# Gate rows of an mLSTM brought to all partitions by transfers from a DRAM scratch instead of matmuls

## The chip, the cores and the metric

One core of a Trainium2 chip runs the whole program. The metric is the device time of one execution in microseconds; a lower time is better.

## What is computed

The reference is a two-layer encoder trunk on 512 tokens of width 1024. Layer 0 mixes tokens with an mLSTM (a chunked, stabilised matrix memory with four heads), layer 1 with causal pooling; each layer then attends to 256 memory tokens and applies a squared-ReLU MLP, and every sub-layer ends in a LayerNorm. The change touches the mLSTM of layer 0 alone. Cut to that:

```python
def mlstm_chunk_step(carry, inp):          # per chunk; q, k, v, input gate, log forget gate
    b = jnp.cumsum(lf, axis=-1)
    dmat = jnp.where(tril, b[..., :, None] - b[..., None, :] + ig[..., None, :], -jnp.inf)
    m_t = jnp.maximum(b + m[..., None], jnp.max(dmat, axis=-1))
    wts = jnp.exp(dmat - m_t[..., None])
    sc = jnp.einsum('bhtd,bhsd->bhts', q, k) * wts
    num = jnp.einsum('bhts,bhsv->bhtv', sc, v) + ...      # the carried state
    h = num / jnp.maximum(jnp.abs(den), jnp.exp(-m_t))[..., None]
```

The kernel does not carry a state over chunks: for each head it forms the whole lower triangle of scores between 512 source and 512 target tokens. So each score needs a weight, the exponential of a number that belongs to the target token (a row, equal on all partitions) plus a number that belongs to the source token (a column, one value for each partition).

## The kernel before

All products run as three matmuls of float32r halves (`mm3`, lines 195 to 200: high by high, high by low, low by high). A weight unit of 128 by 1024 is loaded by SyncE (`unit`, lines 149 to 161), cast to its high half by ScalarE (line 159, tile `wh`), and the rest is found by VectorE (line 160, tile `wl`). There are five buffers each for `wh` and `wl`, and three for the raw loads.

The mLSTM stage begins with nine warm-up matmuls, then `pg`, the gate projection (line 350), then the projections for q and k, `conv(c)` (line 360), each with 24 matmuls, a causal convolution of four taps on ScalarE and VectorE (lines 363 to 365, tile `ac`), a SiLU and a split. Projections for v (`token_proj`, tiles `v`) alternate with the convolutions in the loop over (5, 2, 6, 3, 7): v of token tile 0, then conv(5), v of tile 1, conv(2), v of tile 2, conv(6), and so on. The four units of a v projection stay in their buffers through four token tiles, so that one buffer of five is left for the units of the convolutions in between.

Around these, smaller work is put in by due times: `defer(us, fn)` and `chain(us, step, fns)` (lines 175 to 181) count TensorE time as the program is written out, and `tick` calls what has come due. The order that results is a priority: each engine has its own queue, and the framework that writes the queues out may take a later instruction first where it expects an earlier one not to be ready. Each queue is then run in order.

- `gates()` (line 444), due at 5, makes the input gate and the log forget gate as rows on four partitions (one for each head). For each of the four token tiles s it then makes a segment of the target rows: a running sum (line 458), the source values (line 459), the subtraction of the stabiliser (line 460), and a split into high and low half in `rseg[s]` on partitions 0 to 3 and 32 to 35 (lines 461 and 462). The segments have 512, 384, 256 and 128 columns (`SEG`).
- `columns()` (line 464), due at 21, turns the source values and the stabiliser into columns by eight small transposes (`gcol`, `emcol`).
- `scores(h)` (line 379) has for each s a `weights(s)` and a `part(s)`. `weights(s)` brings row h of the segment to all 128 partitions by a matmul with a selecting matrix (line 385, PSUM tile `pb`; the matrix `sel` is loaded, cast and kept in a buffer of the pool `t2`). VectorE adds the column to the first 128 columns (line 388), GpSimd masks these (line 389), and ScalarE takes the exponential of them (line 390) and of the rest, straight out of PSUM (line 392). `part(s)` makes the scores (PSUM tile `pS`, pool `aux` with two buffers), and VectorE multiplies them by the weights (line 403); a split follows (lines 404, 405). The order is weights 0, weights 1, part 0, weights 2, part 1, weights 3, part 2, part 3, at steps of 2 (head 3: 2.2).
- The `rseg` tiles lie in the four buffers of the pool `lnp`, which the LayerNorm rows of layer 0 use next (`ln_load(0, 0)`, loaded by SyncE).

Of the kernel before, what the change touches and what calls it, by code (L numbers as in the profile page):

```python
# [9 lines left out]
F32 = mybir.dt.float32  # L10
F32R = mybir.dt.float32r
AF = mybir.ActivationFunctionType
ALU = mybir.AluOpType
AX = mybir.AxisListType

P = 128
D = 1024
S = 512
NT = S // P
KC = D // P  # L20
M = 256
H = 4
# [8 lines left out]
SIDE = dict(vkv="left", t5="left", hid="left", t2="right", rawd="right")  # L31
SEG = [S - P * s for s in range(NT)]
OFF = [sum(SEG[:s]) for s in range(NT)]
WU = 1024
LN_T = 7.2


def f32(ap):
    return ap.bitcast(F32)
# [3 lines left out]
def trunk(ctx: ExitStack, tc: tile.TileContext, a: dict, out: bass.AP):  # L43
    nc = tc.nc
    V, A, G, T = nc.vector, nc.scalar, nc.gpsimd, nc.tensor
# [13 lines left out]
    lnp_p = pool("lnp", 1, side="right")  # L59
    st_p = pool("st", 3, side="right")  # L60
    dram_p = pool("dram", 1, space=bass.MemoryType.DRAM)
    acc_p = pool("acc", 4, space=bass.MemoryType.PSUM)
    tmp_p = pool("tmp", 2, space=bass.MemoryType.PSUM)
# [4 lines left out]
    scoped = {}  # L68
# [20 lines left out]
    def ld(dst, src):  # L89
        nc.sync.dma_start(dst, src)  # L90
# [58 lines left out]
    def unit(src):  # L149
# [4 lines left out]
        else:  # L154
            r = raw_p.tile([P, WU], F32, tag="raw", name=f"raw{n}")
        ld(r, src)
        h = wh_p.tile([P, WU], F32R, tag="wh", name=f"wh{n}")
        l = wl_p.tile([P, WU], F32R, tag="wl", name=f"wl{n}")
        A.copy(h, r)  # L159
# [15 lines left out]
    def defer(us, fn):  # L175

        later.append([us, fn])
# [33 lines left out]
    def tok(t):  # L211
        return slice(t * P, (t + 1) * P)
# [122 lines left out]
    for q in range(4):  # L335
        r = vkv(f"xr{q}", F32)[:, : 2 * S].rearrange("p (z t) -> p z t", z=2)
        for z in range(2):
            k = 2 * q + z
            ld(r[:, z], a["xT"][:, k])
            h, l = x0.k(k)  # L340
# [37 lines left out]
    def scores(h):  # L378

        ws = {}  # L380

        def weights(s):
            n = SEG[s]
            pb = tmp_p.tile([P, 512], F32, tag="tmp", name=f"pb{h}{s}")
            T.matmul(pb[:, :n], sel[:, h], rseg[s], start=True, stop=True)
            gc = gcol[:, s, h : h + 1]
            w = ws[s] = t2(f"w{h}{s}", n)
            V.tensor_scalar(w[:, :P], pb[:, :P], gc, None, op0=ALU.add)
            G.affine_select(w[:, :P], w[:, :P], pattern=[[1, P]], compare_op=ALU.is_ge, fill=-1e30, base=0, channel_multiplier=-1)
            A.activation(w[:, :P], w[:, :P], AF.Exp)  # L390
            if n > P:
                A.activation(w[:, P:], pb[:, P:n], AF.Exp, bias=gc, scale=1.0)

        def part(s):
            if s == 0:
                sc[h] = t5(f"sh{h}", F32R), t5(f"sl{h}", F32R)
            w = ws[s]
            q, k = qk_k(h)
            n = SEG[s]
            sh, sl = (z[:, OFF[s] : OFF[s] + n] for z in sc[h])  # L400
            pS = aux_p.tile([P, 512], F32, tag="aux", name=f"pS{h}{s}")
            mm3(pS[:, :n], (k[0][:, tok(s)], k[1][:, tok(s)]), (q[0][:, s * P :], q[1][:, s * P :]), start=True, stop=True)
            V.tensor_tensor(w, pS[:, :n], w, ALU.mult)
            A.copy(sh, w)
            V.tensor_tensor(sl, w, f32(sh), ALU.subtract)

        fns = []
        for s in range(NT):
            fns += [lambda s=s: weights(s), lambda s=s: part(s)]
        order = (0, 2, 1, 4, 3, 6, 5, 7)  # L410
        return [fns[n] for n in order]
# [12 lines left out]
    ld(gateb, a["gateb"])  # L424
    w_v = h_units(a["w_v"][0])
    ident = const_tile("ident", [P, P])
    sel_f = scoped["t2"].tile([P, H, P], F32, tag="t2", name="sel_f")
    ld(sel_f, a["sel"])
    sel = scoped["t2"].tile([P, H, P], F32R, tag="t2", name="sel")
    A.copy(sel, sel_f)  # L430

    ga, gb, bc = t5("ga"), t5("gb"), t5("bc")
    i_r, lf = ga[0:4, 0:512], ga[0:4, 512:1024]
# [3 lines left out]
    m_r, gs_r = gb[0:4, 0:512], gb[0:4, 512:1024]  # L437
    gcol = const.tile([P, NT, H], F32, name="gcol")
    emcol = const.tile([P, NT, H], F32, name="emcol")

    seg = [bc[0:4, OFF[s] : OFF[s] + SEG[s]] for s in range(NT)]
    rseg = [lnp_p.tile([P, 512], F32R, tag=z, name=f"r{z}")[:, : SEG[s]] for s, z in enumerate(("g0", "g1", "b0", "b1"))]

    def gates():
        A.copy(lf, pg[64:68])
        V.scalar_tensor_tensor(i_r, pg[0:4], gateb[0:4], lf, ALU.add, ALU.add)
        A.copy(fe, pg[96:100])
        V.scalar_tensor_tensor(fp, pg[fs], gateb[fs], fe, ALU.add, ALU.add)
        A.activation(fa, fp, AF.Abs)
        A.activation(fe, fa, AF.Exp, scale=-1.0)  # L450
        A.activation(fe, fe, AF.Ln, bias=one_t[fs], scale=1.0)
        V.tensor_scalar(fa, fp, 0.0, None, op0=ALU.min)
        V.tensor_tensor(lf, fa, fe, ALU.subtract)
        V.tensor_tensor_scan(m_r, lf, i_r, 0.0, ALU.add, ALU.max)
        for r in rseg:
            G.memset(f32(r), 0.0)
        for s in range(NT):
            V.tensor_tensor_scan(seg[s], lf[:, s * P :], lf[:, s * P :], 0.0, ALU.add, ALU.bypass)
            V.tensor_tensor(gs_r[:, tok(s)], i_r[:, tok(s)], seg[s][:, :P], ALU.subtract)
            V.tensor_tensor(seg[s], seg[s], m_r[:, s * P :], ALU.subtract)  # L460
            A.copy(rseg[s][0:4], seg[s])
            V.tensor_tensor(rseg[s][32:36], seg[s], f32(rseg[s][0:4]), ALU.subtract)

    def columns():
        pc = tmp_p.tile([P, 512], F32, tag="tmp", name="pc")
# [3 lines left out]
        V.tensor_copy(gcol.rearrange("p a b -> p (a b)"), pc[:, 0:16])  # L469
        A.activation(emcol.rearrange("p a b -> p (a b)"), pc[:, 16:32], AF.Exp, scale=-1.0)  # L470

    defer(5, gates)
    defer(21, columns)
    for j, c in enumerate((5, 2, 6, 3, 7, None, None, None)):
        hf, t = j // 4, j % 4
# [3 lines left out]
        for q in range(2):  # L479
            h = 2 * hf + q  # L480
# [7 lines left out]
    b1 = const_tile("b1", [P, DEPTH, DFF // P])  # L488
# [12 lines left out]
    def head(h):  # L501
# [5 lines left out]
        for t in range(NT):  # L507
            pa = acc_p.tile([P, 512], F32, tag="acc", name=f"pa{h}{t}")
            pn.append(pa)
            for s in range(t + 1):  # L510
                o = OFF[s] + (t - s) * P
                mm3(pa[:, :258], (sh[:, o : o + P], sl[:, o : o + P]), (vh[h][:, s], vl[h][:, s]), start=s == 0, stop=s == t)
# [58 lines left out]
    for q in range(2):  # L571
        r = raw_p.tile([P, 4, M], F32, tag="raw", name=f"mr{q}")
# [84 lines left out]
    for i in range(DEPTH):  # L657
# [255 lines left out]
        for q in range(3, 4):  # L913
            n = f"{i}{q}"
# [24 lines left out]
def _layout(inp):  # L939
    c = np.ascontiguousarray  # L940

    def feat(w):

        k, n = w.shape
        return c(w.reshape(k // P, P, n // P, P).transpose(2, 1, 0, 3)).reshape(n // P, P, -1)

    def half(w):

        k, n = w.shape
        return c(w.reshape(4, 2, P, n // 512, 512).transpose(3, 0, 2, 1, 4)).reshape(n // 512, 4, P, 1024)  # L950

    x, mem = inp["x"][0], inp["mem"][0]
    w_in = inp["mlstm_w_in"][0]
    wg = np.zeros((D, 36), w_in.dtype)
    wg[:, 0:4] = w_in[:, 3072:3076]
    wg[:, 32:36] = w_in[:, 3076:3080]
    gb = np.zeros((36, 1), w_in.dtype)
    gb[0:4, 0] = inp["mlstm_gate_b"][0, 0:4]
    gb[32:36, 0] = inp["mlstm_gate_b"][0, 4:8]
    sel = np.zeros((P, H, P), np.float32)  # L960
    for h in range(H):
        sel[h, h] = 1.0
        sel[32 + h, h] = 1.0
    band = np.zeros((P, 2, 4, BAND), np.float32)
    for w, win in enumerate(WINDOWS):
        for s in range(P):
            for t in range(s, min(s + win, BAND)):
                band[s, 0, w, t] = np.float32(1.0) / np.float32(min(t + 1, win))
                band[s, 1, w, t] = np.float32(1.0 / win)
            band[s, :, w, s] -= np.float32(1.0)  # L970
    w1, w2 = inp["mlp_w1"], inp["mlp_w2"]
    return {
        "ident": np.eye(P, dtype=np.float32),
        "sel": sel,
        "band": band,
        "xT": c(x.T.reshape(KC, P, S).transpose(1, 0, 2)),
        "x": c(x.reshape(NT, P, D).transpose(1, 0, 2)),
        "memT": c(mem.T.reshape(KC, P, M).transpose(1, 0, 2)),
        "w_qk": feat(w_in[:, :1024]),
        "w_v": half(w_in[:, 1024:2048]),  # L980
        "w_o": half(w_in[:, 2048:3072]),
        "wg": c(wg.reshape(KC, P, 36).transpose(1, 0, 2)),
        "gateb": gb,
        "convw": c(inp["mlstm_conv_w"][0].reshape(4, KC, P).transpose(2, 1, 0)),
        "normg": c(inp["mlstm_norm_g"][0].reshape(KC, P).T),
        "w_out": half(inp["mlstm_w_out"][0]),
        "w_pool": c(inp["pool_w"][0].reshape(2, 2, 2, P, 256).transpose(0, 3, 1, 2, 4)).reshape(2, P, 1024),
        "pool_scale": c(inp["pool_scale"]),
        "w_k": feat(inp["mem_w_kv"][:, :D]),
        "w_kvv": half(inp["mem_w_kv"][:, D:]),  # L990
        "w_q": np.stack([feat(w) for w in inp["xattn_wq"]]),
        "w_ao": np.stack([half(w) for w in inp["xattn_wo"]]),
        "w1": np.stack([feat(w) for w in w1]),
        "b1": c(inp["mlp_b1"].reshape(DEPTH, DFF // P, P).transpose(2, 0, 1)),
        "w2": np.stack([np.stack([half(w[q * D : (q + 1) * D]) for q in range(4)]) for w in w2]),
        "b2": c(inp["mlp_b2"]),
        "ln_g": c(inp["ln_g"]),
        "ln_b": c(inp["ln_b"]),
    }
# [18 lines left out]
```

## Time and profile before

| | us |
|---|---|
| three runs | 1207.62, 1210.26, 1210.73 |
| median of the runs | 1210.26 |
| the profiled execution | 1208.14 |
| its span, first to last instruction | 1206.4 |
| TensorE busy in the span | 1191.3 |
| VectorE, ScalarE, GpSimd busy | 835.8, 577.7, 8.9 |

The page gives busy times and the chain of work that ended last. In the timeline of TensorE, matmuls are pipelined: what one costs is the distance from its start to the next start, not its duration. A bracket after a row tells how long the engine stood idle before it and what released it. SyncE issues all loads and stores; GpSimd issues none.

### The profile page before, as it was taken

The page shows a single profiled execution, that of the slowest core. Times are in us where ns is not written, and L with a number is a line of the kernel's source. Part 1 is how long each engine was busy: PE and PEld are TensorE (multiplying, and loading weights), DVE is VectorE, ACT ScalarE, POOL GpSimd, SP SyncE. Part 2 cuts the span into 40 slices and gives each one's busy share as a digit, 9 for nine tenths or more (in the row PEclk, how much of TensorE's full clock was granted, in tenths as well). Part 3 has the DMA queues.
Part 4 walks back from the last instruction along what each step waited for, and adds up shares of the span by engine and source line. Part 5 has one row for each costly group of instructions (what it writes and reads, how often), then busy time and mean ns, then how long its engine had stood idle before and what let it go on. Part 6 is the DMA issues. An engine that isn't in the chain of part 4 may idle for free.

```text
span 1206.4 us, 15476 instructions
## 1 busy us (share of the span) xinstructions
PE 1191.3 (99%) x6121; PEld 1017.5 (84%) x6121; DVE 835.8 (69%) x1145; ACT 577.7 (48%) x853; POOL 8.9 (1%) x35
## 2 busy tenths in 40 slices
PE   9899999999999999999999999999999999999997
PEld 6788889889888988888888889998898888888886
DVE  6776366485548775585698699874868459479746
ACT  6586585233423564454544444562356445454420
POOL 0000000000000000000000000000000000000000
PEclk9999999999999999999999999999999999999999
DMA  7132347624232416116105555544331512511311
GB/s 253 49 117 87 98 131 255 216 89 156 71 140 70 141 44 201 54 50 198 48 10 186 189 194 193 175 123 160 96 112 58 186 53 73 172 35 57 118 53 70
DMA packets 43177, 144.21 MB, mean 120 GB/s; under 512 B 5216, under 2 KB 5472, under 8 KB 43104
## 3 DMA queue, kind: packets, MB, share of 16 engines
q1 hardware_dynamic: 43104, 143.22, 36.2%
q8 instruction: 48, 0.79, 0.3%
q14 instruction: 25, 0.20, 0.0%
HBM read 136.91 MB, written 6.29 MB: 119 GB/s over the span
## 4 chain that ended last, share of the span: by engine, by line
PE 93%; DVE 3%; ACT 1%; DMA 1%; issue 0%; SPq 0%; DVEq 0%; ACTq 0%
PE h L196 10%; PE h L197 10%; PE h L198 10%; PE m L196 7%; PE m L198 7%; PE m L197 7%; PE ao L198 2%; PE ao L196 2%; PE ao L197 2%; PE q L196 2%; PE q L197 2%; PE q L198 2%; PE p L196 2%; PE p L198 2%; PE p L197 2%; PE mo L196 1%
## 5 line engine op out<-in xcount | busy, mean ns | idle before, releaser
L160 DVE TENSOR_TENSOR wl<-raw,wh 128x1024 fp32r<-128x1024 f32 x175 | 213.0, 1222 | 170.6 <-ACT wh L159 168.6
L159 ACT CAST wh<-raw 128x1024 fp32r<-128x1024 f32 x175 | 183.1, 1049 | 281.7 <-PE h L197 74.0
L843 DVE TENSOR_TENSOR b<-b,b 128x1024 f32<-128x1024 f32 x48 | 58.6, 1220 | 0.4
L196 PE MATMUL h<-xm00h,wh 128*128 128x512 f32 (+1 forms) x144 | 52.9, 367 | 0.0
L196 PE MATMUL h<-xm10h,wh 128*128 128x512 f32 (+1 forms) x144 | 52.8, 367 | 0.0
L196 PE MATMUL h<-xm01h,wh 128*128 128x512 f32 (+1 forms) x144 | 52.8, 367 | 0.0
L196 PE MATMUL h<-xm11h,wh 128*128 128x512 f32 (+1 forms) x144 | 52.8, 367 | 0.0
L197 PE MATMUL h<-xm00l,wh 128*128 128x512 f32 (+1 forms) x144 | 52.7, 366 | 0.0
L197 PE MATMUL h<-xm10l,wh 128*128 128x512 f32 (+1 forms) x144 | 52.7, 366 | 0.0
L198 PE MATMUL h<-xm01h,wl 128*128 128x512 f32 (+1 forms) x144 | 52.6, 365 | 0.0
L198 PE MATMUL h<-xm11h,wl 128*128 128x512 f32 (+1 forms) x144 | 52.6, 365 | 0.0
L198 PE MATMUL h<-xm00h,wl 128*128 128x512 f32 (+1 forms) x144 | 52.6, 365 | 0.0
L197 PE MATMUL h<-xm01l,wh 128*128 128x512 f32 (+1 forms) x144 | 52.6, 365 | 0.0
L197 PE MATMUL h<-xm11l,wh 128*128 128x512 f32 (+1 forms) x144 | 52.6, 365 | 0.0
L198 PE MATMUL h<-xm10h,wl 128*128 128x512 f32 (+1 forms) x144 | 52.6, 365 | 0.0
L815 ACT ACTIVATE r<-h,b 128x512 f32<-128x512 f32 x48 | 32.8, 682 | 0.0
L247 ACT ACTIVATE rs<-mv,eps_t 128x1 f32<-128x1 f32 x24 | 7.1, 295 | 53.5 <-DVE mv L245 53.5
L816 ACT ACTIVATE s<-r 128x512 f32<-128x512 f32 x48 | 30.3, 632 | 1.3
L196 PEld LDWEIGHTS h<-xm00h,wh 128*128 128x128 f32 x144 | 27.2, 189 | 4.5 <-ACT r L759 0.2
L197 PEld LDWEIGHTS h<-xm10l,wh 128*128 128x128 f32 x144 | 27.2, 189 | 4.4
L197 PEld LDWEIGHTS h<-xm00l,wh 128*128 128x128 f32 x144 | 27.1, 188 | 4.5
L197 PEld LDWEIGHTS h<-xm01l,wh 128*128 128x128 f32 x144 | 27.2, 189 | 4.4
(946 smaller groups left out, 3527.8 us busy)
## 6 DMA issues: line engine op xcount, KB each, us to landing
raw<-in_w SPq DMA_DIRECT2D x88, 512.0 KB, 3.8
b<-in_w SPq DMA_DIRECT2D x48, 512.0 KB, 4.3
raw<-in_w_q SPq DMA_DIRECT2D x24, 512.0 KB, 4.3
raw<-in_w_ao SPq DMA_DIRECT2D x16, 512.0 KB, 3.5
raw<-in_w_v SPq DMA_DIRECT2D x8, 512.0 KB, 6.0
raw<-in_w_o SPq DMA_DIRECT2D x8, 512.0 KB, 4.2
raw<-in_w_k SPq DMA_DIRECT2D x8, 512.0 KB, 4.2
raw<-in_w_kvv SPq DMA_DIRECT2D x8, 512.0 KB, 4.6
```

What stands on the lines that cost most here:

```text
L159: A.copy(h, r)
L160: V.tensor_tensor(l, r, f32(h), ALU.subtract)
L196: T.matmul(out_, l[0], r[0], start=start, stop=False)
L197: T.matmul(out_, l[0], r[1], start=False, stop=False)
L198: T.matmul(out_, l[1], r[0], start=False, stop=stop)
L247: A.activation(rs, mv[:, 1:2], AF.Sqrt, bias=eps_t, scale=1.0)
L815: A.activation(r, ps, AF.Relu, bias=b1[:, i, 8 * q + m : 8 * q + m + 1], scale=1.0)
L816: A.activation(s[m // 4][:, m % 4], r, AF.Square)
L843: V.tensor_tensor(d, u, v, op)
```

## The change

The rows no longer pass TensorE. `gates()` ends with the stabiliser; what follows for a segment is now `gate_rows(s)`, without the split into halves, and ends with a transfer of the segment (four partitions) into a DRAM scratch `rows`, issued on GpSimd's queue. The five functions are due one by one at 5, 8.5, 12, 15.5 and 19. `weights(s)` fetches row h of the segment 128 times out of the scratch into its buffer `w`, again on GpSimd's queue; the mask follows there, and one exponential with the column as its bias takes the whole width. The matrix `sel`, its load, its cast and its buffer are gone, as are the `rseg` tiles, their clearing on GpSimd, `pb` and its PSUM buffers.

```diff
 def weights(s):
     n = SEG[s]
-    pb = tmp_p.tile([P, 512], F32, tag="tmp", name=f"pb{h}{s}")
-    T.matmul(pb[:, :n], sel[:, h], rseg[s], start=True, stop=True)
-    gc = gcol[:, s, h : h + 1]
     w = ws[s] = t2(f"w{h}{s}", n)
-    V.tensor_scalar(w[:, :P], pb[:, :P], gc, None, op0=ALU.add)
+    G.dma_start(w, rows[h : h + 1, OFF[s] : OFF[s] + n].broadcast_to([P, n]))
     G.affine_select(w[:, :P], w[:, :P], pattern=[[1, P]], compare_op=ALU.is_ge, fill=-1e30, ...)
-    A.activation(w[:, :P], w[:, :P], AF.Exp)
-    if n > P:
-        A.activation(w[:, P:], pb[:, P:n], AF.Exp, bias=gc, scale=1.0)
+    A.activation(w, w, AF.Exp, bias=gcol[:, s, h : h + 1], scale=1.0)
...
-sel_f = scoped["t2"].tile([P, H, P], F32, tag="t2", name="sel_f")
-ld(sel_f, a["sel"])
-sel = scoped["t2"].tile([P, H, P], F32R, tag="t2", name="sel")
-A.copy(sel, sel_f)
...
-rseg = [lnp_p.tile([P, 512], F32R, tag=z, name=f"r{z}")[:, : SEG[s]] for s, z in enumerate(("g0", "g1", "b0", "b1"))]
+rows = dram_p.tile([H, SUM], F32, name="rows")

 def gates():
...
     V.tensor_tensor_scan(m_r, lf, i_r, 0.0, ALU.add, ALU.max)
-    for r in rseg:
-        G.memset(f32(r), 0.0)
-    for s in range(NT):
-        V.tensor_tensor_scan(seg[s], lf[:, s * P :], lf[:, s * P :], 0.0, ALU.add, ALU.bypass)
-        V.tensor_tensor(gs_r[:, tok(s)], i_r[:, tok(s)], seg[s][:, :P], ALU.subtract)
-        V.tensor_tensor(seg[s], seg[s], m_r[:, s * P :], ALU.subtract)
-        A.copy(rseg[s][0:4], seg[s])
-        V.tensor_tensor(rseg[s][32:36], seg[s], f32(rseg[s][0:4]), ALU.subtract)
+
+def gate_rows(s):
+    V.tensor_tensor_scan(seg[s], lf[:, s * P :], lf[:, s * P :], 0.0, ALU.add, ALU.bypass)
+    V.tensor_tensor(gs_r[:, tok(s)], i_r[:, tok(s)], seg[s][:, :P], ALU.subtract)
+    V.tensor_tensor(seg[s], seg[s], m_r[:, s * P :], ALU.subtract)
+    G.dma_start(rows[:, OFF[s] : OFF[s] + SEG[s]], seg[s])
...
-defer(5, gates)
+chain(5, 3.5, [gates] + [lambda s=s: gate_rows(s) for s in range(NT)])
 defer(21, columns)
```

## Rows read from the trace of the kernel before

**Rows 1.** The page: busy time, share of the span, instructions; then the chain by engine.

```profile
PE 1191.3 (99%) x6121; PEld 1017.5 (84%) x6121; DVE 835.8 (69%) x1145; ACT 577.7 (48%) x853; POOL 8.9 (1%) x35
...
PE 93%; DVE 3%; ACT 1%; DMA 1%; issue 0%; SPq 0%; DVEq 0%; ACTq 0%
```

**Rows 2.** What TensorE waited for, whole span: us in total, times, longest.

```profile
PE qk L198 <- DVE wl L160: 3.6, 2, 3.2
...
PE k L196 <- DVE k0l L206: 0.5, 1, 0.5
```

**Rows 3.** TensorE in order of time, 28 to 66 us: start, duration, instruction, [idle before].

```profile
45.97 0.50 PE L196 MATMUL v<-wh,x00h 128*128 128x512 f32 x1
49.64 0.80 PE L198 MATMUL qk<-x00h,wl 128*128 128x512 f32 x1 [3.16 <-DVE wl L160]
...
53.30 0.40 PE L198 MATMUL qk<-x00h,wl 128*128 128x512 f32 x1
```

**Rows 4.** Busy time of each engine, granted clock, DMA share, GB/s, after the wait.

```profile
49.60:53.30 3.70, 3.66 (x9) 2.91 (x10) 2.17 (x5) 2.88 (x5) 0.00 (x0) 0.56 0.40 144
```

**Rows 5.** VectorE by line, 36 to 50 us: count, busy us, mean ns, idle before.

```profile
L458 DVE TENSOR_TENSOR_SCAN bc<-ga 4x512 f32<-4x512 f32 (+3 forms) x4 | 3.1, 796 | 0.0
...
L460 DVE TENSOR_TENSOR bc<-bc,gb 4x512 f32<-4x512 f32 (+3 forms) x4 | 1.9, 472 | 0.1
...
L462 DVE TENSOR_TENSOR rg<-bc,rg 4x512 fp32r<-4x512 f32 (+1 forms) x2 | 1.1, 611 | 0.0
L459 DVE TENSOR_TENSOR gb<-ga,bc 4x128 f32<-4x128 f32 x4 | 1.1, 268 | 0.0
L462 DVE TENSOR_TENSOR rb<-bc,rb 4x256 fp32r<-4x256 f32 (+1 forms) x2 | 0.7, 348 | 0.1
```

**Rows 6.** VectorE in order of time, 10 to 60 us.

```profile
48.37 1.21 DVE L160 TENSOR_TENSOR wl<-raw,wh 128x1024 fp32r<-128x1024 f32 x1
...
57.32 1.22 DVE L160 TENSOR_TENSOR wl<-raw,wh 128x1024 fp32r<-128x1024 f32 x1 [4.85 <-ACT wh L159]
```

**Rows 7.** ScalarE in order of time, 10 to 60 us.

```profile
39.82 1.05 ACT L159 CAST wh<-raw 128x1024 fp32r<-128x1024 f32 x1
```

**Rows 8.** TensorE in order of time around the broadcast matmul of 128 columns.

```profile
74.88 0.22 PE L385 MATMUL pb<-rb,sel 128*128 128x128 f32 x1
...
75.22 0.39 PE L197 MATMUL qk<-x00l,wh 128*128 128x512 f32 x1
```

**Rows 9.** TensorE, 28 to 66 us: first matmuls of conv(6), the first broadcast matmul.

```profile
60.80 0.39 PE L196 MATMUL qk<-x00h,wh 128*128 128x512 f32 x1
...
64.20 0.39 PE L385 MATMUL pb<-rg,sel 128*128 128x512 f32 x1
64.43 0.39 PE L196 MATMUL qk<-x01h,wh 128*128 128x512 f32 x1
```

**Rows 10.** VectorE in order of time, 60 to 170 us.

```profile
66.89 0.35 DVE L388 TENSOR_SCALAR w<-pb,gcol 128x128 f32<-128x128 f32 x1 [1.90 <-PE pb L385]
...
75.59 0.55 DVE L403 TENSOR_TENSOR w<-pS,w 128x384 f32<-128x384 f32 x1
...
117.10 0.35 DVE L388 TENSOR_SCALAR w<-pb,gcol 128x128 f32<-128x128 f32 x1
...
120.13 0.29 DVE L403 TENSOR_TENSOR w<-pS,w 128x128 f32<-128x128 f32 x1 [1.98 <-PE pS L198]
```

**Rows 11.** GpSimd in order of time, 0 to 300 us.

```profile
65.21 0.29 POOL L389 TENSOR_SCALAR_AFFINE_SELECT w<-w 128x128 f32<-128x128 f32 x1 [51.63 <-DVE w L388]
...
72.15 1.15 POOL L389 TENSOR_SCALAR_AFFINE_SELECT w<-w 128x128 f32<-128x128 f32 x1 [4.55 <-DVE w L388]
```

**Rows 12.** SyncE's loads of LayerNorm rows, 128 copies of 2 KB: from issue to landing.

```profile
DMA to landing us min/median/max: 3.7/5.1/6.1
```

**Rows 13.** Chain that ended last, 163 to 180 us: start, duration, what.

```profile
165.88 1.13 DVE meml L576
...
167.04 4.62 DMA raw<-in_w_k
```

More of the change, by code (lines that the diff above doesn't have):

```diff
@@ L33 @@
 OFF = [sum(SEG[:s]) for s in range(NT)]
+SUM = sum(SEG)
 WU = 1024
@@ L959, in _layout @@
     gb[32:36, 0] = inp["mlstm_gate_b"][0, 4:8]
[L960 to L963, printed above, removed]
     band = np.zeros((P, 2, 4, BAND), np.float32)
@@ L973, in _layout @@
         "ident": np.eye(P, dtype=np.float32),
-        "sel": sel,
         "band": band,
```

## Prediction

> **What bounds the kernel now.** I read the page first: TensorE is busy for 1191.3 of 1206.4 us and makes 93% of the chain that ended last, against 835.8 us for VectorE [rows 1]. So a microsecond counts only if it is TensorE's own, or if TensorE stands still for it. The second view is therefore the list of TensorE's waits. It is short: the longest entry, 3.6 us in two pieces, is a matmul of a `conv` that waits for line 160, the low half of its weight unit [rows 2]. The third view is the order of time around the longer piece, and there the reader is to see two things. TensorE starts a matmul at 45.97, then stands still for 3.16 us and starts again at 49.64. Then it is slow: from 49.64 to 53.30 it starts nine matmuls, 3.66 us where nine at the usual distance of 0.23 [rows 9] take 2.07 [rows 3]. The mean granted clock there is 0.56, the lower of the two levels (1.2 instead of 2.4 GHz) for most of the stretch [rows 4]. So this one wait costs 3.16 + 1.59 = 4.75 us.
>
> Fourth, who was late? ScalarE cast the high half of that unit, conv(2)'s, at 39.82, done at 40.87 [rows 7]; VectorE began the low half only at 48.37 [rows 6]. In those 7.5 us VectorE worked nearly without a gap, mostly on the gates: four segments, each a running sum, two subtractions and the low half of `rseg`, all due at one moment ahead of that unit [rows 5]. The wait of TensorE is the gates' doing, and the edit to the gates matters more than the matmuls it was written beside.
>
> **The matmuls.** Sixteen of line 385 go, four for each head, of 512, 384, 256 and 128 columns. One of 512 occupies TensorE for 0.23 us, from 64.20 to 64.43 [rows 9]. At that rate 384 are 0.17 and 256 are 0.115. One of 128 and its successor together take 0.34, from 74.88 to 75.22, where the successor alone takes 0.23; so it costs 0.11 [rows 8]. A head is 0.23 + 0.17 + 0.115 + 0.11 = 0.62, four heads are **2.5 us**, all on the path, since TensorE does not wait once between 60 and 163 us.
>
> **The gates.** Ahead of conv(2)'s unit VectorE loses, first, the four subtractions of line 462, 1.1 + 0.7 = 1.8 us [rows 5]. Second, conv(2)'s unit is written out when 24 matmul triples of v, conv(5) and v have passed, 3 x 8 x 0.64 = 15.4 on the kernel's own count, so the parts due at 15.5 and 19 (segments 2 and 3) now come behind it. The mean segment is 0.80 + 0.47 + 0.27 = 1.54 us [rows 5], two are 3.1; these are the short ones, and by columns they have 384 of 1280, 0.3 x 6.1 = 1.8. I take 2.3. Together 4.1 us: the low half starts at 44.3 instead of 48.37 and ends at 45.5, about 1 us before TensorE ran dry at 46.47 (45.97 + 0.50) [rows 3]. So the wait should go, and with it the slow matmuls: **4.75 us**. What is late next there is `columns()`, whose transposes need all four segments and sit in TensorE's own queue; and the convolution's taps (line 365) share VectorE with it. I give back 0.4 us for that, between 0 and the 3.16 of the old wait, near the other piece of the same wait (3.6 - 3.2) [rows 2].
>
> **What is added.** Twenty transfers on GpSimd's queue. No row shows one issued there. From below, GpSimd's time for one is nothing that matters; from above it is like its slowest instruction, 1.15 us [rows 11]. The nearest row for the landing is SyncE's loads of LayerNorm rows, also 128 copies of 2 KB out of one row: 3.7 to 6.1, median 5.1 us [rows 12]; the shorter ones may be faster. After the landing come the mask (0.29 us for 128 columns [rows 11]) and one exponential of up to 512 columns (between that 0.29 and the 1.05 of a cast of 1024 [rows 7]; I take 0.7), so, with 0.3 for the issue, about 6.4 us from issue to use. How long was there? From line 388 to the multiplication of line 403 I count sixteen pairs, the shortest 3.0 us (117.10 to 120.13), the longest 8.7 (66.89 to 75.59) [rows 10], most between 5 and 7. Issued where the matmul stood, some weights come up to 3 us late and VectorE, which runs in order, waits at line 403; queued behind it are low halves of weights (line 160), and behind those TensorE. But a fetch needs only the stored row and a buffer of `t2`; GpSimd was idle for 51.63 us before its first mask [rows 11], and `t2` gains the buffer that `sel` held. So I expect the fetches to be issued early and most waits to vanish. Bounds: 0, and 3 us for each of four heads. I take 0.8.
>
> Edits with one answer: VectorE loses line 388 (16 x 0.35 = 5.6 us [rows 10]), ScalarE the casts of line 461 and twelve short exponentials; both are beside TensorE and count nothing. SyncE no longer waits for `pb` before it loads the LayerNorm rows; 1 MB may land earlier, in a queue that has room. The stores of the segments are due well ahead of the first fetch.
>
> By the Trainium skill (DMA: Bandwidth & Descriptors, Anatomy of one DMA) a transfer issued by GpSimd takes about 2.0 us plus its bytes at 436 GB/s, so 2.6 us for the largest as an estimate; by it no weight but one would be late, and the sum would lack the 0.8.
>
> **The sum.** 2.5 + 4.75 - 0.4 - 0.8 = 6.05 us off. The profiled execution took 1208.14, of which 1206.4 is its span; it lies 2.1 below the median of the runs (1210.26), near the fastest (1207.62). Against the profiled execution that gives 1202.1; the four times together average 1209.2, which gives 1203.1. I put it at 1203.
>
> **Rivals.** *The wait stays.* The low half is late for another reason, for instance because the taps of conv(5) move into the place left free, or the order of the queues is written out anew with another misjudgement of the same size. For it: the order was wrong by 3 us here once. Against: 4 us of VectorE's work are gone from exactly that place. Then only the matmuls count: 1208.1 - 2.5 = 1205.6, by the mean of the runs 1206.7.
>
> *The fetches are late and TensorE pays (slower).* GpSimd runs in order: fetch, mask (waits for the landing), next fetch. If the mask comes ahead of the next fetch, a head's four weights take 4 x 6 = 24 us, while its parts are due within 14 to 15. The last parts are then 8 us late. Slack: conv(6)'s low half was done at 58.5 (57.32 + 1.22) [rows 6] and used at 60.80 [rows 9], 2.3 us, since only one buffer is left for it. Behind the last head lies the cast of the memory tokens and the load that starts when it is done (165.88, then 167.04 for 4.62 us) [rows 13], after which TensorE waited already (0.5 us) [rows 2], so no slack at all. Lateness of 8 less 2.3 at three places of a convolution (5.7 each, clock aside) would be 17 us; half of them, with 6 us at the memory tokens, 14.5. Less the 7.25 won: 1208.1 + 7.3, by the mean 1216. It decides as soon as more than 7.25 us of new waits reach TensorE. Against: nothing forces mask before fetch.
>
> *GpSimd is held by VectorE.* One mask took 1.15 us in place of 0.29 [rows 11] while VectorE ran line 160. If issuing a transfer suffers likewise, behind a low half of 1.22 us [rows 6] each, a weight is 0.9 to 2 us later, some 1.5 more, and of sixteen perhaps three reach TensorE at 1.2: 3.6 us, 1205.7, by the mean 1206.8. By the Trainium skill (SBUF — State Buffer, Who interferes with whom) a vector instruction with two SBUF inputs contends with reads of GpSimd, and one in a two-port mode locks out the writing of descriptors as well. The row of 1.15 us agrees with the first; by the second this rival needs copies or scalar operations from SBUF to SBUF, which stand hardly anywhere between 60 and 166 us.
>
> **Chances.** The forecast (1200 to 1205.5) 0.58; the wait stays 0.18 (1205 to 1208); GpSimd held 0.08 (1205 to 1208); late fetches 0.16 (1209 to 1222). 0.3%, 3.6 us, is about what a measurement of this kernel can tell from no change, so faster means below 1206.6. Nearly all of the forecast and a little of the two middle cases lie there: faster 0.62, same 0.22, slower 0.16. The range takes in the forecast, with 1 us below it for other small waits that may go (0.4 and 0.5 us [rows 2]), both middle cases and the near part of the slow one: 1199 to 1212.
>
> **What would show it.** Right: no wait of TensorE near 46 us and a granted clock of 1.00 from 30 to 60; no line 385; line 403 following the exponential without waits over 1 us; fetches issued well ahead of their part. Wrong: a wait of `conv` for line 160 as before; waits of lines 389 and 403 that add up, with TensorE waiting for line 160 or for a `pS` buffer between 60 and 180 us.

## The result: 1200.5 us, and where the time went

| | before | changed |
|---|---|---|
| median of the runs, us | 1210.03 (four: 1207.62 to 1210.73) | 1200.47 (four: 1200.29 to 1202.29) |
| profiled execution, us | 1208.14 | 1200.29 |
| its span, us | 1206.4 | 1198.5 |

The recorded ratio is 0.9928, with a 95% interval of 0.9911 to 0.9945. It is that of the two means, 1200.9 and 1209.6 us, which lie 8.7 us apart; the medians lie 9.6 apart. The forecast was 1203.0 with a range of 1199 to 1212. The two profiled executions lie 7.85 us apart.

The page of the changed kernel, busy time and the chain's shares, as [rows 1]:

```profile
PE 1187.2 (99%) x6105; PEld 1014.3 (85%) x6105; DVE 829.0 (69%) x1125; ACT 575.1 (48%) x836; POOL 19.2 (2%) x51
...
PE 95%; DVE 2%; DMA 1%; ACT 1%; issue 0%; SPq 0%; DVEq 0%; ACTq 0%
```

TensorE has 16 matmuls fewer, and its share of the chain rises from 93% to 95%. GpSimd is busy for 19.2 us in place of 8.9: the transfers count there.

What TensorE waited for in the changed kernel, whole span (us in total, times, longest), as [rows 2]:

```profile
PE warm L311 <- POOL zero L308: 1.3, 1, 1.3
PE k L197 <- DVE k0l L207: 1.0, 1, 1.0
...
PE qk L199 <- DVE wl L161: 0.4, 1, 0.4
...
```

The wait of 3.2 us for a unit's low half is gone; the 0.4 left is the first piece, at the start. One entry grew: `k`, from 0.5 to 1.0.

Busy time in the changed kernel from 30 to 60 us and from 60 to 165 (TensorE, its weight loads, VectorE, ScalarE, GpSimd; granted clock, DMA share, GB/s):

```profile
30.00:60.00 30.00, 30.00 (x138) 24.63 (x138) 22.28 (x38) 18.23 (x28) 5.90 (x12) 1.00 0.29 86
60.00:165.00 105.00, 105.00 (x532) 89.26 (x531) 57.51 (x111) 75.90 (x122) 11.58 (x24) 1.00 0.40 115
```

TensorE is busy without a gap in both stretches, at a granted clock of 1.00 (2.4 GHz); of the slow stretch of [rows 4], with 0.56, nothing is left.

The next two fences show why. First TensorE in order of time in the changed kernel: the first matmul of conv(2) and the first after it.

```profile
43.64 0.39 PE L197 MATMUL qk<-x00h,wh 128*128 128x512 f32 x1
...
49.08 0.39 PE L197 MATMUL v<-wh,x00h 128*128 128x512 f32 x1
```

Then VectorE, where the low half of conv(2)'s unit (`wl`) began at 48.37 before [rows 6]:

```profile
42.51 1.21 DVE L161 TENSOR_TENSOR wl<-raw,wh 128x1024 fp32r<-128x1024 f32 x1
43.65 0.73 DVE L366 SCALAR_TENSOR_TENSOR ac<-qk,convw,ac 128x511 f32<-128x511 f32 x1
44.31 0.54 DVE L451 TENSOR_TENSOR bc<-bc,gb 4x384 f32<-4x384 f32 x1
...
46.62 0.41 DVE L449 TENSOR_TENSOR_SCAN bc<-ga 4x128 f32<-4x128 f32 x1
```

The low half now stands ahead of the taps of conv(5) (line 366) and of what is left of segments 1 to 3, and TensorE runs conv(2) through, 24 matmuls in 5.44 us.

To divide the gain I take three marks in every trace: the first copy of the gates on ScalarE, the first matmul on the memory tokens (`memh`), and the last matmul of `mo`, behind which nothing of the change lies. Before and changed (a group of matmuls lists durations in ns, then its first and last start):

```profile
14.44 0.58 ACT L445 COPY ga<-pg 4x512 f32<-4x512 f32 x1 [1.76 <-PE pg L350]
L196 PE MATMUL k<-memh,wh x64: 279/283/385, 170.6 to 200.3; 128*128 128x256 f32 x64
L198 PE MATMUL mo<-wh,y1l x32: 389/389/397, 225.6 to 267.7; 128*128 128x512 f32 x32
```

```profile
13.91 0.58 ACT L437 COPY ga<-pg 4x512 f32<-4x512 f32 x1 [1.85 <-PE pg L351]
L197 PE MATMUL k<-memh,wh x64: 280/283/386, 162.6 to 192.8; 128*128 128x256 f32 x64
L199 PE MATMUL mo<-wh,y1l x32: 389/389/397, 218.2 to 260.2; 128*128 128x512 f32 x32
```

The table gives the same marks for every kernel, us, in the order of the experiments below:

| kernel | first copy | copy to memory tokens | copy to end of `mo` | rest of the span | median of the runs |
|---|---|---|---|---|---|
| before | 14.4 | 156.2 | 253.3 | 938.7 | 1210.0 |
| changed | 13.9 | 148.7 | 246.3 | 938.3 | 1200.5 |
| e1 five parts | 14.7 | 151.3 | 248.2 | 938.3 | 1203.0 |
| e2 one block | 16.3 | 150.8 | 248.1 | 941.6 | 1204.9 |
| e3 idle matmuls | 14.5 | 151.2 | 248.2 | 940.0 | 1205.2 |
| e4 two fetches | 14.3 | 148.7 | 246.4 | 940.0 | 1201.3 |
| e10 three fetches | 14.8 | 153.5 | 251.1 | 939.9 | 1206.1 |
| e5 four fetches | 14.0 | 162.4 | 259.4 | 939.3 | 1215.3 |
| e9 fetch in place | 14.5 | 156.9 | 253.7 | 940.5 | 1212.0 |
| e6 SyncE's queue | 14.0 | 152.3 | 248.5 | 938.8 | 1203.4 |
| e7 six buffers | 14.0 | 148.7 | 246.2 | 938.9 | 1201.2 |
| e8 unchanged again | 14.4 | 148.8 | 246.1 | 939.5 | 1201.4 |

Up to the memory tokens the change takes off 7.5 us, up to the end of `mo` 7.0. The first copy (13.9 to 16.3) and the rest of the span (938.3 to 941.6) differ from execution to execution by 2 to 3 us in places that no edit here touches. So single profiles are compared by the two middle columns, and whole times by medians.

### The profile page after: what moved, and what is told of

Read it like the earlier page. It is cut to its first block, busy times and chain, and to the rows that moved or that the text cites. A ratio compares the mean times of both kernels' runs of the same rounds, so it can differ in the third digit from the quotient of the medians.

```text
span 1198.5 us, 15428 instructions
## 1 busy us (share of the span) xinstructions
PE 1187.2 (99%) x6105; PEld 1014.3 (85%) x6105; DVE 829.0 (69%) x1125; ACT 575.1 (48%) x836; POOL 19.2 (2%) x51
## 4 chain that ended last, share of the span: by engine, by line
PE 95%; DVE 2%; DMA 1%; ACT 1%; issue 0%; SPq 0%; DVEq 0%; ACTq 0%
PE h L198 10%; PE h L197 10%; PE h L199 10%; PE m L199 7%; PE m L197 7%; PE m L198 7%; PE ao L199 2%; PE ao L197 2%; PE ao L198 2%; PE q L197 2%; PE q L198 2%; PE q L199 2%; PE p L197 2%; PE p L198 2%; PE p L199 2%; PE v L197 1%
## 5 line engine op out<-in xcount | busy, mean ns | idle before, releaser
L199 PEld LDWEIGHTS h<-xm01h,wl 128*128 128x128 f32 x144 | 27.2, 189 | 4.4
L197 PEld LDWEIGHTS h<-xm01h,wh 128*128 128x128 f32 x144 | 27.2, 189 | 4.4
```

What stands on the lines that cost most here:

```text
L197: T.matmul(out_, l[0], r[0], start=start, stop=False)
L199: T.matmul(out_, l[1], r[0], start=False, stop=stop)
```

## The experiments

**e1, the gates in five parts and nothing else.** The kernel before, with its matmuls and its `rseg` work.

```diff
-    defer(5, gates)
+    chain(5, 3.5, [gates] + [lambda s=s: gate_rows(s) for s in range(NT)])
```

> The kernel before with one edit: the gates in five parts, due at 5, 8.5, 12, 15.5 and 19; the split of the rows into halves, the selecting matrix and the sixteen broadcast matmuls stay. Theory 1 (the order of VectorE's work ahead of conv(2)'s weight unit made the wait of 3.16 us and the slow clock behind it): the wait is gone, the granted clock is 1.00 from 30 to 60 us, and the time falls by 4.75 us, to about 1205.3 us, ratio 0.996. Rival (the wait goes because the rows are no longer split into halves and ScalarE is spared, or because the matmuls are gone): the wait stays, at 2 to 3 us, and the time is within 1.5 us of the kernel before.

1202.98 us, ratio 0.9943 (0.9931 to 0.9956). The stretch from 30 to 60 us of e1:

```profile
30.00:60.00 30.00, 30.00 (x138) 24.67 (x137) 23.83 (x42) 21.24 (x34) 0.00 (x0) 1.00 0.21 63
```

The wait is gone and with it the slow matmuls: 156.2 - 151.3 = 4.9 us up to the memory tokens, where the wait had been costed at 4.75. The greater part of the gain has nothing to do with DRAM or GpSimd. (The median lies 6.5 us below that of the kernel before; the marks place 4.9 of it here.)

**e2, the changed kernel with the gates in one block.**

```diff
-    chain(5, 3.5, [gates] + [lambda s=s: gate_rows(s) for s in range(NT)])
+    defer(5, all_gates)   # gates(), then gate_rows(0) to gate_rows(3)
```

> The changed kernel with its gates in one block again, all due at 5; the transfers stay. VectorE then has 6.1 us of segment work ahead of conv(2)'s low half instead of about 4, but no subtraction of line 462 of the kernel before (1.8 us). Theory 1: the low half ends near 47.5 us while TensorE wants it near 44.1, so a wait of about 3.4 us comes back, with some 1.6 us of slow clock: 1205.5 us against 1200.5, ratio to the kernel before 0.996. Rival (sparing the split into halves is what removed the wait): no wait over 1 us and a time within 1.5 us of the changed kernel.

1204.94 us, 0.9957 (0.9944 to 0.9971). TensorE in e2 around conv(2), and the windows behind the wait (TensorE, weight loads left out; granted clock, DMA share, GB/s):

```profile
46.25 0.39 PE L198 MATMUL qk<-x00l,wh 128*128 128x512 f32 x1
48.53 0.50 PE L199 MATMUL qk<-x00h,wl 128*128 128x512 f32 x1 [1.90 <-DVE wl L161]
...
48.50:52.20 3.70, 3.67 (x16) 1.00 0.84 225
```

The wait is back, but it lasts 1.90 and the clock stays at 1.00 behind it: 16 matmuls in 3.7 us, against 9 before. Up to the memory tokens e2 loses 2.1 us to the changed kernel, which is what the starts say: 2.28 us from one to the next where 0.23 is usual. So dividing the gates is needed; taking the low halves of `rseg` off VectorE alone would leave 2.1 of the 4.9. A wait of 3.4 us and slow matmuls were expected, and neither came: that the whole time agrees with the expected 1205.5 is luck. The median lies 3.6 to 4.5 above that of the changed kernel (1201.36 in e8, 1200.47); the marks place 2.1 of it here and the rest outside the stretch of the change.

**e3, the changed kernel with sixteen idle matmuls** of the widths of those removed; nobody reads their result.

```diff
+            pb = tmp_p.tile([P, 512], F32, tag="tmp", name=f"pb{h}{s}")
+            T.matmul(pb[:, :n], x0.k(0)[0][:, :P], x0.k(1)[0][:, :n], start=True, stop=True)
             G.dma_start(w, rows[h : h + 1, ...].broadcast_to([P, n]))
```

> The changed kernel with sixteen matmuls added in the places of the removed ones, of the same 512, 384, 256 and 128 columns, into a PSUM tile that nothing reads (operands are two tiles of x; the output does not depend on them). Theory 1: they cost TensorE 0.62 us for each head, 2.5 us in all, and nothing else: 1203.0 us. Rival (a matmul without a reader slips into gaps, or the two PSUM buffers of that pool that they hold delay the transposes): under 1 us, or over 4 us with a wait of TensorE between 60 and 165 us.

1205.21 us, 0.9962 (0.9949 to 0.9974). Up to the memory tokens 151.2 - 148.7 = 2.5 us, the forecast of 2.5; e1, which has the real ones, says 2.6. Up to the end of `mo` it is 1.9 in both, since the wait of `k` is 0.5 in e3 and 0.4 in e1 against 1.0 in the changed kernel: half a microsecond of the matmuls' gain is given back there. The whole time is 2.2 us above the 1203.0 expected, and the medians lie 3.9 to 4.7 apart; TensorE has no wait between 60 and 165 us, and in the profiled executions 0.6 us of the difference lies ahead of the first copy and 1.7 behind `mo`.

**e4, e10, e5, every fetch two, three and four times** into the same place.

```diff
             G.dma_start(w, rows[h : h + 1, ...].broadcast_to([P, n]))
+            G.dma_start(w, rows[h : h + 1, ...].broadcast_to([P, n]))   # once, twice or three times more
```

> The changed kernel with each of the sixteen fetches issued twice into the same buffer, the second after the first has landed: about 3.4 + 0.5 us later for each weight. Theory 1 (fetches are issued long before their part, so they have room): TensorE does not wait more, 1200 to 1202 us. Rival (the fetches are only just in time, the slower rival of the forecast): waits of VectorE at the multiplication grow by up to 4 us each, TensorE waits behind line 161 for several us, 1204 to 1212 us.

> The changed kernel with every fetch made three times into the same place. With two the time was 1201.3 (no new wait), with four 1215.3 (TensorE stood still for 7.5 us at 113.8, waiting for a product whose weight came 9 us late, and ran at the lower clock behind it). If lateness decides from a point on, as the slower rival has it (a queue of about 16 us of GpSimd a head against parts that come every 20 us or so), three times lie between: the fetches of a head take about 3 times 4 us and a weight's lead of 12 to 16 us is used up; no wait to 3 us of waits, 1201 to 1205. If the time were lost in proportion to the number of transfers (a price of each transfer for TensorE), three would be at about 1208, half way between two and four.

> The changed kernel with each of the sixteen fetches issued four times into the same buffer, each after the one before has landed: some 10 to 12 us later for each weight than in the changed kernel. The same with two fetches brought no new wait of TensorE. Theory (the fetches have room of several us, but not of ten): VectorE waits at the multiplication for 2 to 6 us at a time, and from the first gate copy to the first matmul of the memory keys TensorE loses 2 to 10 us: 1203 to 1211 us. Rival (the order of the queues follows any landing, TensorE has other work for so long): no new wait, 1200 to 1202 us.

1201.30, 1206.06 and 1215.26 us (ratios 0.9930, 0.9968, and 1.0044 with 1.0029 to 1.0059). Up to the memory tokens the added transfers cost 0, 4.8 and 13.7 us: nothing at first, then 4.8, then 8.9 more. A price of each transfer for TensorE would have shown in e4 already; this is lateness, which decides from a point on, between two fetches and three. Both guesses missed in size: three cost more than the 3 us of waits allowed, four more than expected. Of the 4.8 and 13.7 us, 3.2 and 10.5 are waits of TensorE between 60 and 165 us.

Each fetch into a tile waits for the landing of the one before, so a weight comes a landing later for every one. What TensorE waited for in e10, 60 to 165 us:

```profile
PE pS L197 <- DVE w L401: 1.3, 1, 1.3
PE o L198 <- DVE wl L161: 1.0, 2, 0.8
PE qk L197 <- DVE w L401: 0.7, 1, 0.7
...
```

In e5, TensorE's last matmul before the longest wait and the first behind it, ScalarE's exponential and VectorE's product that released it, and the window behind (TensorE; granted clock, DMA share, GB/s):

```profile
113.41 0.39 PE L199 MATMUL o<-wh,x01l 128*128 128x512 f32 x1
121.27 0.58 PE L197 MATMUL pS<-qk1h 128*128 128x256 f32 x1 [7.47 <-DVE w L402]
...
119.77 0.72 ACT L391 ACTIVATE w<-w,gcol 128x512 f32<-128x512 f32 x1 [9.37 <-POOL w L390]
...
120.52 0.69 DVE L402 TENSOR_TENSOR w<-pS,w 128x512 f32<-128x512 f32 x1 [9.06 <-ACT w L391]
...
121.20:124.90 3.70, 3.63 (x10) 0.52 0.16 18
```

This is the slower rival at work, place by place: GpSimd's queue late, the exponential late by the mask (line 390), VectorE standing at its product, TensorE standing for a `pS` buffer that the product frees, and the lower clock (0.52, 1.2 GHz) on top after 7.47 us of standing still. The prediction had the chain right. Its sum for this rival put the loss at the low halves of weights; TensorE waits mostly for the `pS` buffer, which the prediction names only among its signs, and for low halves (1.0 us in e10) beside that.

**e9, the fetch held where the matmul stood.** e3 with one column copied from the idle matmul's result into the weight's buffer, so that the fetch cannot go before that matmul.

```diff
             T.matmul(pb[:, :n], x0.k(0)[0][:, :P], x0.k(1)[0][:, :n], start=True, stop=True)
+            A.copy(w[:, :1], pb[:, :1])
             G.dma_start(w, rows[h : h + 1, ...].broadcast_to([P, n]))
```

> The changed kernel with each fetch tied to the place where the matmul stood before: a matmul of the old width whose result nobody needs runs again in the order of TensorE's queue, ScalarE copies one of its columns into the first column of the weight's buffer (the fetch then overwrites it), and the fetch waits for that copy. The output is the reference's. The comparison is with the kernel that has the sixteen idle matmuls but free fetches (1205.2 us; from the first gate copy to the first matmul on the memory tokens 151.2). The prediction gave back 0.8 us, between 0 and 12, for weights that come late, and expected the fetches to go out early because they need nothing but the row and a buffer. If early issue is what saved the time, the exponential now follows the fetch's issue by some 4 us, VectorE waits at its multiplication for the exponential most of the sixteen times, TensorE waits for the product or for a weight's low half, and the time is 2 to 14 us over 1205.2 (1207 to 1219). If early issue did not matter, because the steps between a weight and its product leave 4 us anyway, the time is 1205 to 1206 and the stretch is 151.2 to 152.

1212.03 us (1209.47 to 1213.26), ratio 1.0012 (1.0003 to 1.0022): with the sixteen idle matmuls, which e3 prices at 2.5 us, the whole gain is gone. Against e3, which differs by that column alone, 6.8 us by the medians and 156.9 - 151.2 = 5.7 up to the memory tokens. What VectorE, and then TensorE, waited for in e9 between 60 and 165 us:

```profile
DVE w L402 <- ACT w L391: 14.0, 8, 3.3
...
PE o L197 <- DVE den L506: 0.9, 1, 0.9
PE o L198 <- DVE wl L161: 0.8, 1, 0.8
PE pb L387 <- ACT w L388: 0.6, 1, 0.6
PE pS L197 <- DVE w L402: 0.5, 1, 0.5
PE pS L197 <- ACT w L388: 0.4, 1, 0.4
PE qk L197 <- ACT vh L206: 0.2, 1, 0.2
```

VectorE stands 14.0 us at eight of its sixteen products. TensorE has six waits, 3.4 us together, none above 0.9; two of the six (1.0 us) are for the added copy itself, so lateness alone costs at most 4.7 of the 5.7. The remaining 2.3 lies partly in the restarts, where the distance from the first matmul to the next was up to 0.11 us longer than usual; I could not place all of it. One weight of e9 from issue to product, on GpSimd, ScalarE and VectorE:

```profile
143.76 0.54 POOL L389 DMA_DIRECT2D w<-rows  x1 [23.10 <-ACT w L388]
147.25 0.29 POOL L390 TENSOR_SCALAR_AFFINE_SELECT w<-w 128x128 f32<-128x128 f32 x1 [2.95 <-DMA w<-rows]
147.26 1.28 ACT L391 ACT_TABLE_LOAD   x1 [0.48 <-DMA w<-rows]
148.55 0.73 ACT L391 ACTIVATE w<-w,gcol 128x512 f32<-128x512 f32 x1
149.31 0.69 DVE L402 TENSOR_TENSOR w<-pS,w 128x512 f32<-128x512 f32 x1 [1.06 <-ACT w L391]
```

5.55 us from issue to product, 1.28 of it ScalarE's load of a function table. In the changed kernel the first 3.5 us of this, issue and landing, lie far ahead of the product; only the table load and the exponential stay close to it (63.42 and 64.72 for the first product, at 65.48).

**e6, stores and fetches on SyncE's queue** in place of GpSimd's.

```diff
-            G.dma_start(w, rows[h : h + 1, ...].broadcast_to([P, n]))
+            nc.sync.dma_start(w, rows[h : h + 1, ...].broadcast_to([P, n]))
...
-        G.dma_start(rows[:, OFF[s] : OFF[s] + SEG[s]], seg[s])
+        nc.sync.dma_start(rows[:, OFF[s] : OFF[s] + SEG[s]], seg[s])
```

> The changed kernel with its twenty transfers issued on SyncE's queue, between the loads of weights, in place of GpSimd's. Theory (GpSimd's queue is the right one because nothing else stands in it): fetches wait for a buffer or for a stored segment and hold up loads of w_v and w_o behind them; ScalarE's casts start later, and TensorE waits 1 to 5 us more between 45 and 165 us: 1202 to 1206 us. Rival (any queue does, the loads have room): within 1 us of the changed kernel, 1199.5 to 1201.5.

1203.40 us, 0.9945 (0.9928 to 0.9963). Up to the memory tokens it loses 3.6 us to the changed kernel, 2.8 of them as waits between 60 and 165. The longest, with what ScalarE did ahead of it:

```profile
154.63 0.44 PE L197 MATMUL pS<-qk1h 128*128 128x384 f32 x1 [1.95 <-ACT og L487]
...
145.65 1.28 ACT L388 ACT_TABLE_LOAD   x1 [1.99 <-DMA w<-rows]
...
150.86 1.28 ACT L388 ACT_TABLE_LOAD   x1
152.16 0.51 ACT L388 ACTIVATE w<-w,gcol 128x256 f32<-128x256 f32 x1
152.69 1.28 ACT L487 ACT_TABLE_LOAD   x1
153.98 0.60 ACT L487 ACTIVATE og<-o 128x512 f32<-128x512 f32 x1
```

TensorE stands for a PSUM buffer that ScalarE frees with the output gate (`og`), behind an exponential and two table loads. The changed kernel has the same sequence there and no wait. What made ScalarE late is in its own rows: it stood still for the landing of a fetch before the table loads of its exponentials at 134.32 (2.78 us) and 145.65 (1.99 us), and nowhere in the same stretch of the changed kernel. In e6 SyncE issued the last three fetches only from 141.60 on, in the changed kernel GpSimd had issued all sixteen by 112.24. So the fetches came late from SyncE's queue and ScalarE paid; a late fetch from GpSimd's queue at that time was not tried by itself.

**e7, the pool `t2` back to six buffers**, without the one that `sel` had held (`t2=7` to `t2=6`).

> The changed kernel with six buffers in the pool t2 instead of seven, that is without the buffer that the selecting matrix gave back. Theory (the early issue of the fetches lives on the buffers of t2): fetches are issued later and the convolutions wait for buffers; up to 2 us of new waits of TensorE, 1200 to 1203 us. Rival (the buffer was not needed): no change, 1200 to 1201.5 us.

1201.17 us, 0.9926 (0.9909 to 0.9943), 148.7 up to the memory tokens: the same. The sixteen fetches went out between 48.57 and 114.01 us, against 48.45 and 112.24 in the changed kernel, so early issue does not hang on the buffer that became free.

**e8, the changed kernel again**, without any edit, to see how far two executions lie apart.

> The changed kernel once more, unchanged. If the differences in the first 14 us (the landing of the first loads) and in the pooling stage (waits of po near 745 us) belong to the execution and not to the edits, they differ here from the first profile of the same kernel by up to 2 us, while the stretch from the first gate copy to the first matmul of the memory keys stays at 148.7 us within 0.3.

1201.36 us, 0.9927 (0.9907 to 0.9947). The middle columns agree within 0.3 us with the first profile, the first copy and the rest of the span only within 0.4 and 1.2.

## Why the prediction was right, point by point

**The matmuls** (2.5): 2.5 measured (e3).

**The gates' wait** (4.75): 4.9 measured (e1). The 3.16 us of standing still are counted from the end of a matmul; by starts, as one matmul follows another, the wait is 49.64 - 45.97 - 0.23 = 3.44, and with the 1.59 of slow matmuls 5.0. The working inside was off in one term that happened to help. The low half was forecast for 44.3 and came at 42.51; with the first copy 0.53 earlier in this execution, that is 5.3 us earlier than before in place of 4.1. The four subtractions of line 462 (1.85 us, forecast 1.8) and what of segments 1 to 3 now stands behind the unit (0.54 + 0.27 + 0.40 + 0.41 + 0.28 + 0.28 = 2.2, forecast 2.3) were sized well, although it was not segments 2 and 3 whole: the running sum of 2 stayed ahead and the subtraction of 1 went behind. Missing from the sum were two taps of conv(5), 1.5 us by line 365's durations (0.73 and 0.75), that had stood ahead of the unit before and now stand behind it. The first rival had feared the opposite, that the taps would fill the place. It did not come to pass. e2 shows that the four subtractions alone would not have done it: with the gates in one block the low half is late again.

**The give-back of 0.4 for `columns()` and the taps**: nothing. TensorE has no wait between 30 and 60 us.

**The give-back of 0.8 for late fetches**: nothing on TensorE. This term was mis-sized, and the reason stands in the prediction beside it: the fetches went out early. GpSimd in the changed kernel:

```profile
41.27 0.66 POOL L452 DMA_DIRECT2D rows<-bc  x1 [28.32 <-DVE bc L451]
...
48.45 1.12 POOL L386 DMA_DIRECT2D w<-rows  x2
52.55 0.29 POOL L387 TENSOR_SCALAR_AFFINE_SELECT w<-w 128x128 f32<-128x128 f32 x1 [2.98 <-DMA w<-rows]
...
78.14 1.33 POOL L387 TENSOR_SCALAR_AFFINE_SELECT w<-w 128x128 f32<-128x128 f32 x1 [0.46 <-DMA w<-rows]
...
112.24 0.53 POOL L386 DMA_DIRECT2D w<-rows  x1 [1.82 <-DVE sl L401]
```

The first fetch goes out at 48.45 and its product begins at 65.48; head 1's first at 69.65 for 84.83; the last at 112.24 for 157.68. Fetches stand in pairs and fours ahead of their masks, so a head never pays four landings in a row. The forecast of no wait above 1 us at the product missed twice, and it cost TensorE nothing; VectorE in the changed kernel, 60 to 165 us:

```profile
DVE w L399 <- ACT w L388: 2.4, 2, 1.3
```

e9 shows what the term would have been without early issue: at most 4.7 us, inside the bounds of 0 and 12 that were given for it; 2.5 + 4.9 - 0.5 - 4.7 would have left 2.2 us, less than the 3.6 that the prediction asks of a change. In the working beside it two readings are off, and nothing hangs on them: of the sixteen pairs eight, not most, lie between 5 and 7 us, and the matmul at 60.80 reads conv(6)'s high half; its low half is first read at 61.26, so that the slack was 2.7 us and not 2.3.

**The landing and the issue.** The estimate was 5.1 us to land, from SyncE's loads of LayerNorm rows [rows 12], and 0.3 for the issue. The weights' fetches in the changed kernel (issue in ns: least, median, most; then issue to landing):

```profile
L386 POOL DMA_DIRECT2D w<-rows x16: 534/544/573, 48.5 to 112.2; - x16
...
DMA to landing us min/median/max: 3.1/3.4/4.5
```

The landing was shorter, the issue longer, and each issue occupies GpSimd for its 0.54 us. By size the medians are 3.7 us for 256 KB and 3.4 for 64 KB. By the Trainium skill (DMA: Bandwidth & Descriptors, Anatomy of one DMA) it is 2.0 us plus the bytes at 436 GB/s, which as an estimate is 2.6 and 2.2; the traces show 1.1 and 1.2 more. Nothing in the result hangs on that difference, since the fetches lead by 15 us and more.

**GpSimd held by VectorE.** One mask took 1.33 us in place of 0.29, as in [rows 11]: it began at 78.14 and ended at 79.47, VectorE's line 161 ran from 78.10 to 79.31. No issue took more than 0.57 (0.66 for the first store), also where one fell beside line 161, as at 91.51 (0.53, line 161 from 90.79 to 92.01). So what slows the mask did not slow the issuing of transfers here, and this rival falls. The Trainium skill (SBUF — State Buffer, Who interferes with whom) also has VectorE's two-port modes locking out the writing of descriptors. No issue in these traces shows it; VectorE ran no copy or scalar operation from SBUF to SBUF while the transfers went out, so it was not tested.

**What was not in the sum.** The wait of `k` on the memory tokens grew from 0.5 to 1.0 us. The prediction named that place, where the load of `w_k` starts behind the last head, as one without slack. The chain there, 155 to 172 us of the changed kernel, as [rows 13]:

```profile
157.96 1.14 DVE meml L566
...
159.12 5.07 DMA raw<-in_w_k
```

The load took 5.07 us where it took 4.62. But the wait goes with the matmuls, not with one landing: it is 0.8 to 1.0 in six profiles without the sixteen matmuls (changed, e2, e4, e7, e8, e10) and 0.3 to 0.5 in four with them (before, e1, e3, e9); e5 (0.5) and e6 (none) had lost their time shortly before. By what path the matmuls shorten it, no run shows.

**Edits with one answer.** They went as said: TensorE did not notice line 388 and the short exponentials, and SyncE now issues the LayerNorm rows from 15.38 on in place of 145.13, with no new wait of TensorE behind them.

**The sum.** Forecast 2.5 + 4.75 - 0.4 - 0.8 = 6.05. Measured to the end of `mo`: 2.5 + 4.9 - 0.5 = 6.9, which is 0.85 more: 1.2 of give-backs that were not needed and 0.15 more for the gates' wait, less the 0.5 at `k`. The marks give 7.0. With 0.5 from an earlier first copy and 0.4 from the rest of the span that is the 7.9 between the two spans. The means and medians of the runs differ by 1.7 and 2.6 us more than the traces explain up to `mo`; the profiled execution of before was a fast one of its kind (1208.14 against a median of 1210.0), and which of its stretches are longer in the other runs no trace shows.

## What to carry to other kernels

Look at what stands ahead of a late operand in its engine's queue before counting the work that a change removes: dividing one block of small work, so that a weight's low half could pass it, brought twice what the removed matmuls did, and could be had without any transfer (e1). A transfer in place of a matmul was free here because its issue was not tied to the place of the matmul; the same fetches held in place cost up to 4.7 us, nearly twice what the removed matmuls had (e9). Count in lateness, not in transfers: a second fetch cost nothing, a fourth 8.9 us more than a third.

## What the runs showed of the hardware

A transfer on GpSimd's queue occupied GpSimd for 0.52 to 0.57 us (0.66 at most) and, as 128 copies of one row out of DRAM, landed 3.1 to 4.5 us after its issue in the changed kernel; on SyncE's queue (e6) the same fetches took 2.9 to 7.0, median 4.1.

TensorE's granted clock fell to 0.56 and 0.52, the lower level for most of the stretch, after it had stood still for 3.16 us (before) and 7.47 us (e5); after 1.90 us (e2) and 1.95 us (e6) it stayed at 1.00. So the wait in e2, 1.3 us shorter than that of before, cost 2.1 us in place of 4.9.
